# Expert products scattered in float32, one slot buffer, and a second late ring buffer

## The chip, the cores and the metric

The kernel runs on one core of one Trainium2 chip. The metric is the device time of one execution in microseconds (us). Before the change it is 1568.03 us, the median of three runs (1567.27 to 1569.21).

## The reference

Four transformer layers are computed for 256 tokens of width 1024. The first two layers (`first_block`) have a token mixer and a mixture of 32 experts; the last two (`second_block`) have other mixers and a dense feed-forward part. The change touches the experts of the first two layers alone:

```python
def hierarchical_moe(h, w_grp, b_grp, w_exp, b_exp, w_gate, w_up, w_down):
    ...
    g_idx = jnp.argmax(grp_logits, axis=-1)
    ...
    top_logit, top_idx = lax.top_k(in_grp, TOP_K)          # TOP_K = 2 of 8 experts of one group
    weights = jax.nn.softmax(top_logit, axis=-1) * p_grp
    expert_id = g_idx[:, None] * EXPERTS_PER_GROUP + top_idx
    combine = ...                                          # token x 32 experts, two non-zero per token
    for gi in range(N_GROUPS):
        hid = silu(t @ w_gate[e]) * (t @ w_up[e])          # for the 8 experts e of the group
        y = y + (hid * combine[e]) @ w_down[e]
```

Each expert has a gate matrix and an up matrix of 1024 x 256 and a down matrix of 256 x 1024, 1 MB each in float32. One layer so reads 96 MB of expert weights.

## The kernel before

**Experts.** Each expert gets 32 slots (`CAP`), and four experts make a block of 128 slots. `moe` walks over nine blocks, `BLOCKS = 0..6, "x", 7`; block "x" gives 32 more slots to the expert with the most tokens. For a block, `slots` picks the tokens with one-hot matmuls (`gp`, evicted by ACT into `xsl`), `gate_up` runs the gate and up products (L1095, tile `gu`, 32-row tiles of four experts side by side) and makes `P`, the one-hot matrix slots x tokens (L1106). `turn` transposes the hidden values (`hdt`, `hT`), `down` runs the down products (L1136, tile `dn`, two halves of 512 columns), and `scatter` adds them at their tokens with matmuls against `P` into four accumulators `ya` (L1153). The last lines of `moe` add `ya` to the residual `x` on DVE (L1188).

**The scatter's precision.** `down` splits each half of `dn` in two parts of type float32r: ACT copies the half into `ys0` (L1140), and DVE writes the remainder `dn - ys0` into `ys1` (L1141). `scatter` runs one float32r matmul for each part, so two for each of the eight slices `k` of 128 columns. In the trace a float32r matmul is one MATMUL record and a float32 matmul is two: the 1024 float32 matmuls of L1095 with the tile `xsl` are listed x2048, and the 288 float32r ones of L1153 x288. Each record is called a pass here.

**The ring of weight buffers.** All weights come through one in-order list of DMAs on SP (class `Ring`, L213), 1 MB each as a rule. A DMA is issued when a buffer is free. There are 8 base buffers and 3 more; during the experts of a layer come `NX` = 6 more from the space of the mixer, and `NY` = 1 more (`extend(1, NY, there)`), once the projection before the experts has given up its space. That is 18. The list goes, for the experts, gate x4, up x4 of block 0, gate x4, up x4 of block 1, down x4 of block 0, and so on.

**Order of the work.** The engines' queues are filled by a scheduler at build time, which interleaves the matmuls of neighbouring steps. `overflow` stands under a test on the device for the case that an expert has more tokens than slots; it is skipped in the profiled execution (no instruction of its body is in the trace), but every engine reads the count and takes the branch (L1194, L1195), between block 6 and block "x".

**Space.** The pool of a layer's experts has tags with a number of buffers each: `k1=3`, `k2=2`, `x4=2`, `k8=1`. `x4` holds `xsl`, 4 KB a partition for each buffer; a ring buffer takes 8 KB a partition.

Of the kernel before, what the change touches and what calls it, by code (L numbers as in the profile page):

```python
# [10 lines left out]
F32 = mybir.dt.float32  # L11
R32 = mybir.dt.float32r
U32 = mybir.dt.uint32
I32 = mybir.dt.int32
AF = mybir.ActivationFunctionType
# [11 lines left out]
NB = 8  # L27
NM = 3
NX = 6
NY = 1  # L30
LAST = 2, 3
K2 = 9
K3 = 2
# [195 lines left out]
class K:  # L229
# [791 lines left out]
    def moe(self, l, ps, sb, gate, last):  # L1021
# [64 lines left out]
        def gate_up(b, info, xs):  # L1086
            es = members(b)
            n = CAP * len(es)
            gu = ps.tile([128, 2, 256], F32, name="gu", tag="ps")
            for m, name in enumerate(("mg", "mu")):  # L1090
                w = [self.W.get((name, l, e)).rearrange("p (k f) -> p k f", k=KD) for e in es]
                for k in range(KD):
                    for j in range(len(es)):
                        q = slice(CAP * j, CAP * j + CAP)
                        nc.tensor.matmul(gu[q, m], xs[:, k, q], w[j][:, k],  # L1095
                                         start=k == 0 and m == 0, stop=k == KD - 1 and m == 1,
                                         tile_position=(0, CAP * j))
                for e in es:
                    self.W.done((name, l, e))
            inf = info() if callable(info) else info  # L1100
            sg = sb.tile([128, 256], F32, name="sg", tag="k1")
            nc.scalar.activation(sg[:n], gu[:n, 0], AF.Silu)  # L1102
            hid = sg
            nc.vector.scalar_tensor_tensor(hid[:n], sg[:n], inf[:, 1:2], gu[:n, 1], op0=OP.mult, op1=OP.mult)  # L1104
            P = sb.tile([128, T], R32, name="P", bufs=3)
            nc.vector.tensor_scalar(P[:n], c("iota1")[:n], inf[:, 0:1], None, op0=OP.is_equal)  # L1106
            Ps[b] = P
            return hid
# [9 lines left out]
        def down(b, halves=(0, 1)):  # L1118
# [7 lines left out]
                keys = [[("md", l, e) for e in es]] * 2  # L1126
                w = [[self.W.get(k)[:, 1024 * n:1024 * n + 1024] for k in keys[0]] for n in range(2)]
            if 0 in halves:
                ys[b] = [sb.tile([128, KD, 128], R32, name=f"ys{j}", bufs=1) for j in range(2)]
            y = ys[b]  # L1130
            for n in halves:
                dn = ps.tile([128, 512], F32, name="dn", tag="ps")
# [4 lines left out]
                                         start=j == 0, stop=j == 1, tile_position=(0, CAP * i))  # L1137
                v = dn[:m].rearrange("s (k p) -> s k p", k=4)
                s = slice(4 * n, 4 * n + 4)
                nc.scalar.activation(y[0][:m, s], v, AF.Copy)  # L1140
                nc.vector.tensor_tensor(y[1][:m, s], v, y[0][:m, s], op=OP.subtract)  # L1141
                if b == 7:
                    for k in dict.fromkeys(keys[n]):
                        self.W.done(k)
# [4 lines left out]
        def scatter(b, ks=range(KD)):  # L1149
            m = CAP * len(members(b))  # L1150
            for k in ks:
                for j in range(2):
                    nc.tensor.matmul(ya[k // 2][:, k % 2], ys[b][j][:m, k], Ps[b][:m],  # L1153
                                     start=b == BLOCKS[0] and j == 0 and k % 2 == 0,
                                     stop=b == BLOCKS[-1] and j == 1 and k % 2 == 1)

        cur = slots(0)
        most, cap, number, px, wx = weights()
# [32 lines left out]
    def overflow(self, l, ps, sb, ht, tw, place, most, cap, ya):  # L1191
# [3 lines left out]
        with self.tc.If(n > 0):  # L1195
# [6 lines left out]
            ov = sb.tile([128, 2, 32], F32, name="ov")  # L1202
            nc.vector.tensor_tensor(ov, place, cap.unsqueeze(1).to_broadcast([128, 2, 32]), op=OP.is_gt)
            nc.vector.tensor_tensor(ov, ov, tw[:, :, 1:], op=OP.mult)
            hid = sb.tile([128, 2, T], F32, name="ohid", tag="x4")

            def part(src):
                t = sb.tile([128, 512], F32, name="ow", tag="k2")
# [1 line left out]
                return t  # L1210

            for e in range(NE):
                wb = ps.tile([128, T], F32, name="wb", tag="ps")
                for cc in range(2):
                    nc.tensor.matmul(wb[:, 128 * cc:128 * cc + 128], ov[:, cc, e:e + 1].to_broadcast([128, 128]),
                                     c("ident"), start=True, stop=True)
                gu = [ps.tile([128, 2, T], F32, name="ogu", tag="ps") for _ in range(2)]
                for m, name in enumerate(("wg", "wu")):
                    src = self.A[name][l, e].rearrange("(p k) f -> p (k f)", p=128)
                    for k in range(KD):  # L1220
                        if k % 2 == 0:
                            v = part(src[:, 256 * k:256 * k + 512]).rearrange("p (k j f) -> p k j f", k=2, j=2)
                        for j in range(2):
                            nc.tensor.matmul(gu[m][:, j], v[:, k % 2, j], h(k), start=k == 0 and j == 0,
                                             stop=k == KD - 1 and j == 1)
                nc.scalar.activation(hid, gu[0], AF.Silu)
                nc.vector.tensor_tensor(hid, hid, gu[1], op=OP.mult)
                nc.vector.tensor_tensor(hid, hid, wb.unsqueeze(1).to_broadcast([128, 2, T]), op=OP.mult)
                for n in range(2):
                    for j in range(2):  # L1230
                        o = 1024 * n + 512 * j
                        v = part(self.A["wd"][l, e][:, o:o + 512]).rearrange("f (k p) -> f k p", k=4)
                        for k in range(4):
                            nc.tensor.matmul(ya[2 * n + k // 2][:, k % 2], v[:, k], hid[:, j], start=False, stop=False)

    def final_norm(self, ps, sb, sc, sh, hl):

# [262 lines left out]
    def run(self, out):  # L1500
# [26 lines left out]
        for l in range(2):  # L1527
# [36 lines left out]
            self.out_proj(ps, ("wout", l), self.hl, gate, self.router(l, ps))  # L1564
            self.split.close()
            assert not self.chunks and not self.parts
            es, sb = self.phase(f"moe{l}", there, k1=3, k2=2, x4=2, k8=1)
            if NY:
                extend(1, NY, there)
            gate = mlp_gate  # L1570
# [307 lines left out]
```

## Time and profile before

| | us |
|---|---|
| median of three runs | 1568.03 |
| lowest, highest | 1567.27, 1569.21 |
| the profiled execution, whole | 1566.22 |
| its span, first to last instruction | 1564.1 |
| PE busy (matmul) | 1447.1 |
| DVE busy | 824.1 |
| ACT busy | 656.1 |

The experts of the first layer lie at 221 to 445 us of the span, those of the second at 647 to 871 us. [...] PE busy is no measure of how full PE is, since matmuls overlap; a timeline row that starts after the one ahead of it has ended shows an idle PE, and in square brackets what ended the idle time.

### The profile page before, as it was taken

To read this page: it belongs to the slowest core of one execution; us is meant where nothing else is said; L and a number is where in the kernel's file an instruction comes from. 1 tells how busy PE (TensorE), PEld (TensorE's weight loads), DVE (VectorE), ACT (ScalarE), POOL (GpSimd) and SP (SyncE) were. 2 spreads that over 40 slices of the span, in tenths; PEclk is the share of its full clock that TensorE was granted. 3 is DMA by queue.
4 is the path that set the end of the run, shared out by engine and by line. 5 is a ranking of instruction groups with operands and counts; after the bars stand their busy time and mean duration, and the time that the engine had idled before them with its cause. 6 is when DMAs were issued, how large, how long until landed. Compare 5 with 4: busy or idle time off the path is not lost. (4 is left out here: it accounts for less than half of the span.)

```text
span 1564.1 us, 28414 instructions
## 1 busy us (share of the span) xinstructions
PE 1447.1 (93%) x11988; PEld 1143.9 (73%) x11988; DVE 824.1 (53%) x1580; ACT 656.1 (42%) x1098; POOL 3.0 (0%) x11
## 2 busy tenths in 40 slices
PE   4999999878989999897889999999999999899997
PEld 2868876434457778754445688799996997799996
DVE  3585631100157755311011667888846675788853
ACT  3534522111144254321121486566634544466643
POOL 0000000000000000000000000000000000000000
PEclk8999999989989999999899999999999999999999
DMA  9976789999998368899999877955546644655520
GB/s 379 420 278 243 277 326 421 421 421 420 416 393 348 121 243 329 333 420 420 421 420 415 335 291 283 375 190 186 176 159 245 244 162 157 221 193 185 189 82 28
DMA packets 64954, 453.02 MB, mean 290 GB/s; under 512 B 7088, under 2 KB 7728, under 8 KB 11440
## 3 DMA queue, kind: packets, MB, share of 16 engines
q1 hardware_dynamic: 63520, 446.94, 73.5%
q10 hardware_dynamic: 1296, 4.15, 0.7%
q8 instruction: 98, 1.61, 0.4%
q14 instruction: 40, 0.33, 0.1%
HBM read 450.01 MB, written 1.05 MB: 288 GB/s over the span
## 5 line engine op out<-in xcount | busy, mean ns | idle before, releaser
L517 PE MATMUL pj<-act,wh 128*128 128x256 f32 x3136 | 582.1, 287 | 20.3 <-ACT act L464 12.6
L517 PEld LDWEIGHTS pj<-act,wh 128*128 128x128 f32 x3136 | 494.8, 194 | 55.9 <-ACT act L464 15.3
L517 PE MATMUL pj<-act,wl 128*128 128x256 f32 x1568 | 446.2, 285 | 0.6 <-DVE wl L510 0.6
L510 DVE TENSOR_TENSOR wl<-wt,wh 128x1024 fp32r<-128x1024 f32 x260 | 317.2, 1223 | 222.7 <-ACT wh L509 220.0
L509 ACT ACTIVATE wh<-wt 128x1024 fp32r<-128x1024 f32 x260 | 274.3, 1059 | 345.8 <-PE pj L517 269.4
L517 PEld LDWEIGHTS pj<-act,wl 128*128 128x128 f32 x1568 | 303.3, 193 | 3.0 <-issue 1.2
L1095 PE MATMUL gu<-wt,xsl 128*32 128x256 f32 x2048 | 148.5, 410 | 36.8 <-DMA wt<-in_wu 33.8
L1095 PEld LDWEIGHTS gu<-wt,xsl 128*32 128x32 f32 x2048 | 72.4, 117 | 103.2 <-DMA wt<-in_wu 44.9
L517 PE MATMUL fd<-F,wh 128*128 128x256 f32 x704 | 125.0, 281 | 0.0
L1136 PE MATMUL dn<-wt,hT 128*32 128x512 f32 x528 | 114.5, 613 | 0.9 <-ACT hT L1116 0.9
L299 PE MATMUL ad<-wt,cz 128*32 128x512 f32 x768 | 112.9, 614 | 0.0
L517 PEld LDWEIGHTS fd<-F,wh 128*128 128x128 f32 x704 | 107.8, 188 | 0.2 <-ACT wh L509 0.2
L1104 DVE SCALAR_TENSOR_TENSOR sg<-sg,inf,gu 128x256 f32<-128x256 f32 x16 | 7.7, 480 | 180.6 <-ACT sg L1102 180.5
L517 PE MATMUL fd<-F,wl 128*128 128x256 f32 x352 | 98.6, 281 | 0.0
L1102 ACT ACTIVATE sg<-gu 128x256 f32<-128x256 f32 (+1 forms) x18 | 6.9, 382 | 212.5 <-PE gu L1095 206.1
L567 DVE SCALAR_TENSOR_TENSOR u<-pj,par,u 128x255 f32<-128x255 f32 (+1 forms) x176 | 84.3, 479 | 3.0
L1058 ACT ACTIVATE xsl<-gp,mod,gsm 128x128 f32<-128x128 f32 x128 | 48.1, 456 | 57.0 <-PE gp L1055 57.0
L1055 PEld LDWEIGHTS gp<-G,ht 128*128 128x128 f32 x512 | 62.2, 200 | 11.0 <-issue 11.0
L1055 PE MATMUL gp<-G,ht 128*128 128x128 f32 x512 | 65.7, 285 | 1.6 <-DVE G L1033 1.6
L517 PEld LDWEIGHTS fd<-F,wl 128*128 128x128 f32 x352 | 66.3, 188 | 0.0
L1136 PEld LDWEIGHTS dn<-wt,hT 128*32 128x32 f32 x528 | 26.4, 111 | 51.7 <-issue 43.2
L1153 PEld LDWEIGHTS ya<-P,ys 128*128 128x128 f32 (+1 forms) x288 | 36.9, 188 | 28.7 <-issue 12.8
(395 smaller groups left out, 1524.0 us busy)
## 6 DMA issues: line engine op xcount, KB each, us to landing
wt<-in_ada SPq DMA_DIRECT2D x96, 1024.0 KB, 6.9
wt<-in_wg SPq DMA_DIRECT2D x66, 1024.0 KB, 19.8
wt<-in_wu SPq DMA_DIRECT2D x66, 1024.0 KB, 19.8
wt<-in_wd SPq DMA_DIRECT2D x66, 1024.0 KB, 19.8
wt<-in_fup SPq DMA_DIRECT2D x44, 1024.0 KB, 4.9
wt<-in_win SPq DMA_DIRECT2D x26, 1024.0 KB, 12.9
wt<-in_fdn SPq DMA_DIRECT2D x22, 1024.0 KB, 4.8
wt<-in_glain SPq DMA_DIRECT2D x12, 1024.0 KB, 6.9
```

The source lines that it names most:

```text
L299: nc.tensor.matmul(acc[32 * g:32 * g + 32], cz[:, k, :], w[:, 512 * g:512 * g + 512], start=k % 4 == 0, stop=k % 4 == 3, tile_position=(0, ...
L509: nc.scalar.activation(wh, raw, AF.Copy)
L510: nc.vector.tensor_tensor(wl, raw, wh, op=OP.subtract)
L517: nc.tensor.matmul(out, lhs[a], rhs[b], start=first and i == 0, stop=last and i == 2)
L567: nc.vector.scalar_tensor_tensor(out[:, d:], src[:, :T - d], w(taps - 1 - d), out[:, d:], op0=OP.mult, op1=OP.add)
L1055: nc.tensor.matmul(gp[:, kk], ht[:, k + kk, cc], G[:, cc].rearrange("p a b -> p (a b)"), start=kk == 0 and cc == 0, stop=kk == 3 and cc == 1)
L1058: nc.scalar.activation(xs[:, kk], gp[:, kk - k], AF.Identity, scale=self.gs[:, kk:kk + 1], bias=self.sh[:, kk:kk + 1])
L1095: nc.tensor.matmul(gu[q, m], xs[:, k, q], w[j][:, k], start=k == 0 and m == 0, stop=k == KD - 1 and m == 1, tile_position=(0, CAP * j))
L1102: nc.scalar.activation(sg[:n], gu[:n, 0], AF.Silu)
L1104: nc.vector.scalar_tensor_tensor(hid[:n], sg[:n], inf[:, 1:2], gu[:n, 1], op0=OP.mult, op1=OP.mult)
L1136: nc.tensor.matmul(dn[q], hT[b][:, j, q], w[n][i][:, 512 * j:512 * j + 512], start=j == 0, stop=j == 1, tile_position=(0, CAP * i))
L1153: nc.tensor.matmul(ya[k // 2][:, k % 2], ys[b][j][:m, k], Ps[b][:m], start=b == BLOCKS[0] and j == 0 and k % 2 == 0, stop=b == BLOCKS[-1] ...
```

## The change

The down products are kept as one float32 tile `ys` (4 KB a partition in place of two tiles of 4 KB), half of each bank copied by ACT and half by DVE. `P` becomes float32, and `scatter` runs one float32 matmul for each slice in place of two float32r ones. The tag `x4` goes from two buffers to one. `NY` goes from 1 to 2, which makes 19 ring buffers during the experts. In the skipped `overflow` the hidden tile moves to a tag of 1 KB a partition, and its loops run over halves of the tokens; that part is cut here.

```diff
-NY = 1
+NY = 2
...
-            P = sb.tile([128, T], R32, name="P", bufs=3)
+            P = sb.tile([128, T], F32, name="P", bufs=3)
...
-                ys[b] = [sb.tile([128, KD, 128], R32, name=f"ys{j}", bufs=1) for j in range(2)]
+                ys[b] = sb.tile([128, KD, 128], F32, name="ys", bufs=1)
...
-                nc.scalar.activation(y[0][:m, s], v, AF.Copy)
-                nc.vector.tensor_tensor(y[1][:m, s], v, y[0][:m, s], op=OP.subtract)
+                nc.scalar.activation(y[:m, s][:, :2], v[:, :2], AF.Copy)
+                nc.vector.tensor_copy(y[:m, s][:, 2:], v[:, 2:])
...
             for k in ks:
-                for j in range(2):
-                    nc.tensor.matmul(ya[k // 2][:, k % 2], ys[b][j][:m, k], Ps[b][:m],
-                                     start=b == BLOCKS[0] and j == 0 and k % 2 == 0,
-                                     stop=b == BLOCKS[-1] and j == 1 and k % 2 == 1)
+                nc.tensor.matmul(ya[k // 2][:, k % 2], ys[b][:m, k], Ps[b][:m], start=b == BLOCKS[0] and k % 2 == 0,
+                                 stop=b == BLOCKS[-1] and k % 2 == 1)
...
-            hid = sb.tile([128, 2, T], F32, name="ohid", tag="x4")
+            hid = sb.tile([128, 2, 128], F32, name="ohid", tag="k1")
...
-            es, sb = self.phase(f"moe{l}", there, k1=3, k2=2, x4=2, k8=1)
+            es, sb = self.phase(f"moe{l}", there, k1=3, k2=2, x4=1, k8=1)
```

How the queues stand, at three places of the first layer (the second has the same ones).

SP, the loads just before and after the first gate and up products (`wt` are ring buffers; in brackets the engines and DMA queues whose signals a load waits for). Before:

```order
L213 DMA wt_2056<-in_wu 128x2048 [waits DMAHW5_49,PE_49]
L213 DMA wt_2062<-in_wu 128x2048 [waits DMAHW6_49]
L213 DMA wt_2071<-in_wu 128x2048 [waits DMAHW7_49,PE_49]
L213 DMA wt_2077<-in_wu 128x2048 [waits DMAHW0_49,PE_49]
L213 DMA wt_2083<-in_wd 128x2048 [waits DMAHW1_49,PE_49]
L213 DMA wt_2151<-in_wd 128x2048 [waits DMAHW2_49,PE_49]
L213 DMA wt_2255<-in_wd 128x2048 [waits DMAHW3_49,PE_49]
L213 DMA wt_2257<-in_wd 128x2048 [waits DMAHW4_49,PE_49]
```

SP, the same loads with the change:

```order
L213 DMA wt_2056<-in_wu 128x2048 [waits DMAHW5_49,PE_49]
L213 DMA wt_2058<-in_wu 128x2048 [waits DMAHW6_49]
L213 DMA wt_2064<-in_wu 128x2048 [waits DMAHW7_49]
L213 DMA wt_2073<-in_wu 128x2048 [waits DMAHW0_49,PE_49]
L213 DMA wt_2079<-in_wd 128x2048 [waits DMAHW1_49,PE_49]
L213 DMA wt_2085<-in_wd 128x2048 [waits DMAHW2_49,PE_49]
L213 DMA wt_2153<-in_wd 128x2048 [waits DMAHW3_49,PE_49]
L213 DMA wt_2257<-in_wd 128x2048 [waits DMAHW4_49,PE_49]
```

The third load needs no signal of PE now, since the second late buffer is there for it, and each load behind it takes the release that the one behind it took before; two buffers (2255, 2257) were handed out after the first gate products before, and one (2257) now.

PE, the last down products and scatters, from the second half of block 7 on. Before:

```order
L1136 MATMUL dn<-wt_6122,hT 32x512
L1153 MATMUL ya<-P,ys_6269 128x256 x2
L1136 MATMUL dn<-wt_6122,hT 32x512
L1136 MATMUL dn<-wt_6124,hT 32x512 x2
L1136 MATMUL dn<-wt_6122,hT 32x512
L1153 MATMUL ya<-P,ys_6270 128x256
L1153 MATMUL ya<-P,ys_6269 128x256
L1153 MATMUL ya<-P,ys_6270 128x256 x2
L1153 MATMUL ya<-P,ys_6269 128x256
L1153 MATMUL ya<-P,ys_6270 128x256
L1136 MATMUL dn<-wt_6122,hT 32x512
L1136 MATMUL dn<-wt_6124,hT 32x512 x2
```

PE, with the change, from the transpose of block 7 to the end of its scatter:

```order
L1114 MATMUL hdt<-cst_71,sg 128x128 x2
L1136 MATMUL dn<-wt_3327,hT 32x512 x2
L1136 MATMUL dn<-wt_3329,hT 32x512 x2
L1136 MATMUL dn<-wt_3327,hT 32x512 x2
L1136 MATMUL dn<-wt_3329,hT 32x512 x2
L1136 MATMUL dn<-wt_8563,hT 32x512
L1152 MATMUL ya<-P,ys 128x256 x4
L1136 MATMUL dn<-wt_8563,hT 32x512
L1136 MATMUL dn<-wt_8565,hT 32x512 x2
L1136 MATMUL dn<-wt_8563,hT 32x512 x2
L1136 MATMUL dn<-wt_8565,hT 32x512 x2
L1152 MATMUL ya<-P,ys 128x256 x4
```

The first half's scatter is one piece of four float32 matmuls (eight passes) where two pieces of float32r matmuls stood on both sides of three down products, and the second half's scatter is four matmuls.

ACT, the end of the experts and the start of the next norm (`warm` is a small activation behind the load of a function table, `nsq` the squares for the norm). Before:

```order
L1116 ACTIVATE hT<-hdt 128x256 [waits PE_49]
L1140 ACTIVATE ys_6269<-dn 128x512 [waits DVE_49,PE_49]
L1140 ACTIVATE ys_6269<-dn 128x512 [waits PE_49]
L412 ACT_TABLE_LOAD
L412 ACTIVATE warm<-x,eps 128x1 [waits DVE_49]
```

ACT, with the change:

```order
L1116 ACTIVATE hT<-hdt 128x256 [waits PE_49]
L1140 ACTIVATE ys<-dn 128x256 [waits DVE_49,PE_49]
L412 ACT_TABLE_LOAD
L412 ACTIVATE warm<-x,eps 128x1 [waits DVE_49]
L1140 ACTIVATE ys<-dn 128x256 [waits PE_49]
```

The table load and `warm` now stand between the two copies of block 7. DVE's copies of the other halves, with the change, wait for ACT:

```order
L1104 SCALAR_TENSOR_TENSOR sg<-sg,inf,gu 128x256 [waits Activation_49]
L1141 COPY ys<-dn 128x256 [waits Activation_49]
L1186 SCALAR_TENSOR_TENSOR x<-ya,mod_171,x 128x256 [waits PE_49]
L1186 SCALAR_TENSOR_TENSOR x<-ya,mod_171,x 128x256
L1186 SCALAR_TENSOR_TENSOR x<-ya,mod_171,x 128x256 [waits PE_49]
```

## Rows read from the trace of the kernel before

**Rows 1.** Stretches of 10 us: five engines busy, clock, DMA share, GB/s.
```profile
310.00:320.00 10.00, 4.94 (x56) 2.05 (x52) 0.00 (x0) 0.00 (x0) 0.00 (x0) 0.87 1.01 419
...
820.00:830.00 10.00, 10.00 (x52) 5.44 (x51) 1.67 (x4) 0.60 (x1) 0.00 (x0) 0.66 1.02 424
```
**Rows 2.** SP's waits at the first gate products, both layers: us, times, longest.
```profile
SPq L213 <- PE gu L1095: 12.6, 1, 12.6
...
SPq L213 <- PE gu L1095: 10.5, 1, 10.5
```
**Rows 3.** One stretch of 1 us, columns as in Rows 1.
```profile
226.00:227.00 1.00, 1.00 (x19) 0.60 (x21) 0.00 (x0) 0.72 (x3) 0.00 (x0) 1.00 0.06 25
```
**Rows 4.** PE's timeline at the last waits for weights, both layers.
```profile
379.02 5.03 PE L1095 MATMUL gu<-wt,xsl 128*32 128x256 f32 x57 [1.51 <-DMA wt<-in_wu]
...
803.83 5.95 PE L1095 MATMUL gu<-wt,xsl 128*32 128x256 f32 x57 [1.89 <-DMA wt<-in_wu]
```
**Rows 5.** PE's timeline from the branch to block 7, first layer.
```profile
404.79 0.35 PE L1153 MATMUL ya<-P,ys 128*128 128x256 f32 x1 [3.40 <-PEq L1195]
405.07 8.78 PE L1095 MATMUL gu<-wt,xsx 128*32 128x256 f32 x32
413.78 2.05 PE L1153 MATMUL ya<-P,ys 128*128 128x256 f32 x15
415.76 3.64 PE L1136 MATMUL dn<-wt,hT 128*32 128x512 f32 x32
...
419.57 1.46 PE L1153 MATMUL ya<-P,ys 128*128 128x256 f32 x10
420.95 1.04 PE L1136 MATMUL dn<-wt,hT 128*32 128x512 f32 x2
...
432.44 2.16 PE L1153 MATMUL ya<-P,ys 32*128 32x256 f32 x16
```
**Rows 6.** PE's timeline, second layer: block 7, then the next norm.
```profile
863.81 0.50 PE L1153 MATMUL ya<-P,ys 128*128 128x256 f32 x2
864.24 1.06 PE L1136 MATMUL dn<-wt,hT 128*32 128x512 f32 x8
865.24 0.98 PE L1153 MATMUL ya<-P,ys 128*128 128x256 f32 x6
866.14 1.06 PE L1136 MATMUL dn<-wt,hT 128*32 128x512 f32 x6
867.13 1.05 PE L311 MATMUL adt<-cst,adrow 128*128 128x4 f32 x8
...
870.36 1.16 PE L381 MATMUL nm<-nsq,fin 128*32 128x256 f32 x6 [0.72 <-ACT nsq L416]
...
875.11 1.03 PE L384 MATMUL nm<-nsq,cst 128*128 128x256 f32 x4
875.97 1.03 PE L384 MATMUL nm<-nsq,fin 128*128 128x256 f32 x4
```
**Rows 7.** Timeline at the end of the first layer's experts, ACT and PE.
```profile
441.61 0.60 ACT L1140 ACTIVATE ys<-dn 128x512 fp32r<-128x512 f32 x1 [3.56 <-PE dn L1136]
442.23 1.28 ACT L412 ACT_TABLE_LOAD   x1
...
442.26 0.51 PE L1153 MATMUL ya<-P,ys 128*128 128x256 f32 x2 [0.73 <-ACT ys L1140]
...
444.68 0.63 PE L381 MATMUL nm<-nsq,cst 128*32 128x256 f32 x4 [0.72 <-ACT nsq L416]
```
**Rows 8.** Groups by form: busy us, mean ns of one | idle before.
```profile
L1141 DVE TENSOR_TENSOR ys<-dn,ys 128x512 fp32r<-128x512 f32 x32 | 22.1, 692 | 47.8 <-ACT ys L1140 47.8
L1116 ACT ACTIVATE hT<-hdt 128x256 f32<-128x256 f32 x16 | 6.1, 383 | 23.9 <-PE hdt L1114 23.9
```
**Rows 9.** The branch L1195 by engine: count, ns min/median/max, first and last start.
```profile
L1195 PEldq COMPARE_BRANCH x2: 6059/6089/6119, 398.5 to 824.8; - x2
```
**Rows 10.** PE's timeline behind the branch, second layer.
```profile
832.45 1.89 PE L1095 MATMUL gu<-wt,xsx 128*32 128x256 f32 x8 [1.07 <-DVEq L1195]
```

More of the change, by code (lines that the diff above doesn't have):

```diff
@@ L1212, in overflow @@
             for e in range(NE):
-                wb = ps.tile([128, T], F32, name="wb", tag="ps")
                 for cc in range(2):
[L1215 to L1222, printed above, removed]
-                        for j in range(2):
-                            nc.tensor.matmul(gu[m][:, j], v[:, k % 2, j], h(k), start=k == 0 and j == 0,
-                                             stop=k == KD - 1 and j == 1)
@@ L1226, in overflow @@
[L1226 to L1234, printed above, removed]
+                    t = slice(128 * cc, 128 * cc + 128)
@@ new lines, in overflow @@
+                    wb = ps.tile([128, 128], F32, name="wb", tag="ps")
+                    nc.tensor.matmul(wb, ov[:, cc, e:e + 1].to_broadcast([128, 128]), c("ident"), start=True, stop=True)
+                    gu = [ps.tile([128, 2, 128], F32, name="ogu", tag="ps") for _ in range(2)]
+                    for m, name in enumerate(("wg", "wu")):
+                        src = self.A[name][l, e].rearrange("(p k) f -> p (k f)", p=128)
+                        for k in range(KD):
+                            if k % 2 == 0:
+                                v = part(src[:, 256 * k:256 * k + 512]).rearrange("p (k j f) -> p k j f", k=2, j=2)
+                            for j in range(2):
+                                nc.tensor.matmul(gu[m][:, j], v[:, k % 2, j], h(k)[:, t], start=k == 0 and j == 0,
+                                                 stop=k == KD - 1 and j == 1)
@@ new lines, in overflow @@
+                    nc.scalar.activation(hid, gu[0], AF.Silu)
+                    nc.vector.tensor_tensor(hid, hid, gu[1], op=OP.mult)
+                    nc.vector.tensor_tensor(hid, hid, wb.unsqueeze(1).to_broadcast([128, 2, 128]), op=OP.mult)
+                    for n in range(2):
+                        for j in range(2):
+                            o = 1024 * n + 512 * j
+                            v = part(self.A["wd"][l, e][:, o:o + 512]).rearrange("f (k p) -> f k p", k=4)
+                            for k in range(4):
+                                nc.tensor.matmul(ya[2 * n + k // 2][:, k % 2, t], v[:, k], hid[:, j], start=False,
+                                                 stop=False)
```

## The prediction

> **What bounds the kernel now.** I read the stretches of 10 us first, to find which engine is full where the experts run, then SP's waits, then PE's timeline through the experts' end. The change touches the experts of two layers and nothing else, so their stretches are all that counts. In the middle of a layer's experts the DMA engines are full (share 1.01, 419 GB/s), and PE is busy for 4.94 of 10 us [rows 1]: the loads set the pace. That ends with the last load that PE waits for, the up weights of block 6. PE waits for one at 379.02 us and at 803.83 us for the last time in each layer [rows 4]. From there on PE's rows follow each other nearly without a hole: the branch, block "x", the scatters of blocks 5, 6 and "x", and block 7 [rows 5, 6]. So a layer's experts have three parts. At first PE works on what was loaded ahead; then the loads decide; and in the last 65 us PE decides, with the short chain ACT, DVE, PE at the end [rows 7]. A saving or a cost counts in full if it moves the last awaited load, or lies in PE's last part.
>
> **The buffer.** SP waits 12.6 us in the first layer and 10.5 us in the second for PE to release the first gate buffers [rows 2], and the DMA engines run dry meanwhile (share 0.06 in a stretch of that time [rows 3]). Six loads go out between the end of the projection and that release now. The order of SP's queue shows a seventh with the change: the third load needs no signal of PE any more, and all behind it move up by one release. One load of 1.05 MB at 419 GB/s [rows 1] is 2.5 us. Nothing dries up after that point, so each later load lands one load earlier, the last awaited one too: 2.5 us for each layer, **5.0 us gained**. The bounds are 0, if the queue stays empty for as long all the same, and 2.5 us for each layer, since one buffer can't bring more than one load. I take the upper one, because the empty time in the rows (12.6 and 10.5 us of waiting) is longer than a load.
>
> **The scatter.** A float32r matmul is one pass, and a float32 one is two. The nearest row for a float32 pass of 128 x 256 over all 128 rows is in the next norm: four passes of L384 start 0.86 us before the next four [rows 6], 0.215 us each. Sixteen passes, so one block's scatter, cost 3.44 us. Before, they cost what the starts of the rows that follow show [rows 5, 6]:
>
> Block 5: 0.28 us for the first (404.79 to 405.07) and 1.98 us for fifteen (413.78 to 415.76), 2.26 us; more by 1.18 us.
> Block 6: 1.38 us for ten (419.57 to 420.95) and six as in 865.24 to 866.14, 0.90 us; more by 1.16 us.
> Block "x": 2.16 us; more by 1.28 us.
> Block 7, first half: 0.43 us (863.81 to 864.24) and 0.90 us; eight passes now cost 1.72 us, more by 0.39 us.
>
> That is 4.0 us for each layer in PE's last part, and the shapes repeat in both, so **8.0 us lost**. [...] The scatters of blocks 0 to 4 get longer by the same 1.2 us each, some 6 us a layer. They cost nothing as long as PE idles for half of the time there [rows 1]; without that cover they would cost 12 us in all.
>
> **The end of the chain.** The second half of block 7 was: down products end (0.08 us before 441.61), ACT copies 0.60 us, PE starts the scatter at 442.26, ACT loads a table for 1.28 us, and PE starts the sums for the norm at 444.68 us, after 0.72 us of waiting for ACT's squares [rows 7]. That is 3.15 us from the end of the down products. Now ACT copies 128 x 256 of it, half of the tile, in 0.38 us by the nearest row [rows 8]. The table load stands ahead of it, where ACT idled for 3.56 us [rows 7], so it is covered, and the squares of the first four slices are ready before PE has ended its scatter. PE needs 0.08 + 0.38 + 0.05 us to start and 1.72 us for eight passes, 2.23 us. So the sums start **0.9 us** earlier in the first layer. If `warm`, which waits for the first slice of `x`, were late, ACT's copy would be late behind it, and the gain would be gone. In the second layer PE does the turn of a row (`adt`) first: it ends near 868.1 us, the scatter would end at 869.8, and the sums started at 870.36 [rows 6]: **0.5 us** gained.
>
> **DVE's copy and the branch.** DVE copied the remainder for 692 ns [rows 8] after ACT's 597; now it copies a half. The order shows that this copy waits for ACT, so the two halves run one after the other, 0.38 and some 0.35 to 0.45 us in place of 0.60 and 0.69: 0.5 us less ahead of the branch. In the first layer that hides: PE's own branch takes 6.06 us [rows 9] and lets PE start at 404.79, later than DVE. In the second PE waits 1.07 us for DVE's branch [rows 10], so **0.5 us** are gained there.
>
> [...]
>
> [...]
>
> **At nothing.** One buffer for `xsl` in place of two: the next block's products into it stand behind the gate and up products of this block in PE's queue in both orders, so no engine waits more. `P` in float32 has the same size. The skipped body of `overflow` gets longer, which costs nothing unless the 6.06 us of the branch depend on the distance. One pair of loads changes places in the second mixer, where PE waits for no load.
>
> **The sum.** -5.0 + 8.0 - 0.9 - 0.5 - 0.5 = +1.1 us. The profiled execution took 1566.2 us, so it would take 1567.3; the median of the runs lies 1.8 us above it, which makes **1569.1 us**. A measurement of this kernel can tell about 0.2%, 3.1 us, from no change, so this is no change.
>
> **Rivals.**
> *The lead is lost (slower).* The place is SP's queue ahead of the first gate products. If the added load waits for the same release as before, or if the loads behind it start later by as much, the last awaited load lands when it did, and the scatters' cost stays: +1.1 + 5.0, so 1574.1 us, 0.4% slower. It decides if fewer than seven loads go out before that release. For it: the order names only engines that a load waits for, not which of their instructions. Against it: the buffer handed out after the first products is one now, where it was two.
> *The clock stays up (faster).* PE runs at half speed after some waits: the last 57 up products take 5.03 and 5.95 us [rows 4], where four experts side by side at 0.215 us would need 3.1 us (57 / 4 x 0.215), and the 32 products behind the branch, of one expert and so one after the other, take 8.7 us [rows 5], 0.27 us each against 0.215. In 820 to 830 us the clock is at 0.66 though PE is busy all the time [rows 1]. These stretches cost some 1.9, 2.8, 1.8 and 3.4 us, 9.9 us in all. More passes mean fewer holes. If half of it went, 5.0 us would be gained: 1564.1 us. Against it: the holes before the last awaited load shrink from about 5 to 4 us only, and where a drop falls may turn out worse as well.
> *The middle scatters show too.* If PE falls behind the loads, all eighteen scatters count: 12 us more, 1581 us. Against it stands the idle half of PE in [rows 1].
>
> **How the numbers follow.** The forecast has a chance of 0.52, the lost lead 0.20, the clock 0.18, the middle scatters 0.05, and 0.05 is left for what I don't see. Within 0.2% means 1564.9 to 1571.2 us. Most of the forecast lies in it (0.46 of 0.52), and 0.04 of the rest: same 0.50. Slower gets the lost lead, the middle scatters and 0.05 more: 0.30. Faster gets most of the clock's chance and some of the rest: 0.20. The range runs from the clock's case to the lost lead's, 1564 to 1574.5 us.
>
> **What would show it.** In the trace after, seven loads before the first gate products, the last wait for up weights 2.5 us earlier against the start of the experts, passes of L1152 at 0.215 us, one scatter of 3.4 us for each of the blocks 5, 6 and "x", and the sums for the norm 2.2 us behind the last down products. The prediction is wrong if that last wait hasn't moved, if PE waits for a load behind it, or if half-speed stretches in the last part differ by more than 3 us in sum from those before.

## The result: 1% slower, far outside the range

The changed kernel takes 1584.2 us (median of four runs, 1577.9 to 1585.9) against 1567.7 us for the kernel before (four runs): a ratio of 1.0097, 95% interval 1.008 to 1.0114. The forecast was 1569.1 us, the range ended at 1574.5 us. The profiled execution has a span of 1581.1 us, 17.0 us more than before.

Where the 17 us came from is read by marks that both traces have: the first rank products of a layer (`rkp`, they start its experts), the last up products that wait for weights, and the first sums for the next norm.

Rank products on PE's timeline of the kernel before (start us, us, ...), both layers:
```profile
218.71 0.38 PE L970 MATMUL rkp<-oh,cst 128*128 128x32 f32 x2 [1.82 <-DVE w L984]
...
644.79 0.38 PE L970 MATMUL rkp<-oh,cst 128*128 128x32 f32 x2 [1.30 <-DVE w L984]
```
The same marks in the changed kernel, with the last waits for weights and the sums for the norm:
```profile
221.19 0.38 PE L970 MATMUL rkp<-oh,cst 128*128 128x32 f32 x2 [1.83 <-DVE w L984]
...
379.27 5.92 PE L1095 MATMUL gu<-wt,xsl 128*32 128x256 f32 x57 [1.87 <-DMA wt<-in_wu]
...
453.45 0.62 PE L381 MATMUL nm<-nsq,cst 128*32 128x256 f32 x4 [0.72 <-ACT nsq L416]
...
653.63 0.38 PE L970 MATMUL rkp<-oh,cst 128*128 128x32 f32 x2 [1.30 <-DVE w L984]
...
809.82 5.68 PE L1095 MATMUL gu<-wt,xsl 128*32 128x256 f32 x57 [1.65 <-DMA wt<-in_wu]
...
888.63 0.62 PE L381 MATMUL nm<-nsq,fin 128*32 128x256 f32 x4 [0.72 <-ACT nsq L416]
```
With [rows 4, 6, 7] for the kernel before, the differences of these starts are:

| stretch | before | after | change |
|---|---|---|---|
| start to the first layer's rank products | 218.7 | 221.2 | +2.5 |
| first layer: rank products to the last awaited weights | 160.3 | 158.1 | -2.2 |
| first layer: from there to the sums for the norm | 65.7 | 74.2 | +8.5 |
| up to the second layer's rank products | 200.1 | 200.2 | +0.1 |
| second layer: to the last awaited weights | 159.0 | 156.2 | -2.9 |
| second layer: from there to the sums for the norm | 66.5 | 78.8 | +12.3 |
| to the end of the span | 693.7 | 692.5 | -1.3 |

So the lead is there, 5.1 us for both layers, and the loss is in PE's last part, where +3 us were forecast for each layer (4.0 for the passes, less the end of the chain and the branch). Two things in that part weren't in the sum.

**A hole behind the branch.** PE's timeline of the changed kernel in the second layer, from the scatter of block 5 on:
```profile
837.02 0.46 PE L1152 MATMUL ya<-P,ys 128*128 128x256 f32 x1 [0.82 <-PEq L1193]
842.70 0.59 PE L1152 MATMUL ya<-P,ys 128*128 128x256 f32 x1 [5.23 <-issue]
843.22 9.71 PE L1095 MATMUL gu<-wt,xsx 128*32 128x256 f32 x32
```
The branch has ended, one pass of the first scatter has run, and its second pass comes 5.23 us later. "Issue" means that the profile shows nothing that it waits for. Block x's products then take 9.7 us, in good part at half speed (granted clock 0.50 from 843 to 848 us, below), where 7.1 us are enough at full speed (a row of the run with the shift, below).

**The clock.** Stretches of the kernel before: both last parts, and block x's scatter with 6 us behind it (us, engines busy, granted clock with 1.00 as full speed, DMA share, GB/s):
```profile
379.02:444.68 65.66, 59.84 (x464) 31.74 (x464) 12.01 (x28) 12.04 (x26) 0.52 (x1) 0.95 1.02 417
803.83:870.36 66.53, 63.26 (x473) 33.58 (x473) 12.09 (x29) 12.04 (x26) 0.00 (x0) 0.91 1.02 418
432.00:440.00 8.00, 7.53 (x55) 3.71 (x51) 1.17 (x2) 1.36 (x3) 0.00 (x0) 1.00 1.03 415
```
The same of the changed kernel, with 8 us up to the fall, the fall beside block x's scatter, and the one behind the hole:
```profile
379.27:453.45 74.18, 70.78 (x464) 37.03 (x464) 10.46 (x29) 10.33 (x26) 0.52 (x1) 0.87 1.01 418
809.82:888.63 78.81, 71.29 (x472) 38.19 (x473) 10.54 (x30) 10.33 (x26) 0.00 (x0) 0.88 0.88 352
431.00:439.00 8.00, 8.00 (x107) 5.38 (x96) 0.48 (x1) 0.38 (x1) 0.00 (x0) 1.00 1.03 415
439.00:445.00 6.00, 5.53 (x22) 1.71 (x21) 0.00 (x0) 0.38 (x1) 0.00 (x0) 0.50 1.01 419
...
843.00:848.00 5.00, 5.00 (x13) 2.00 (x13) 0.00 (x0) 0.00 (x0) 0.00 (x0) 0.50 1.03 426
```
A stretch times what is missing of its clock is an estimate of what the clock took, and an upper one, since an idle PE loses nothing by it: 3.3 and 6.0 us before, 9.6 and 9.5 us after, so up to 9.8 us more. One fall is plain to see: at 439 us, 3 us after block x's scatter began, the clock goes from 1.00 to 0.50, though PE had been busy without a gap for 8 us.

### The profile page after: what moved, and what is told of

Its sections match the earlier page's. It is cut to its first block, busy times and chain, and to the rows that moved or that the text cites. A ratio compares the mean times of both kernels' runs of the same rounds, so it can differ in the third digit from the quotient of the medians.

```text
span 1581.1 us, 28422 instructions
## 1 busy us (share of the span) xinstructions
PE 1475.3 (93%) x11988; PEld 1160.9 (73%) x11988; DVE 815.1 (52%) x1580; ACT 648.1 (41%) x1098; POOL 3.0 (0%) x11
## 3 DMA queue, kind: packets, MB, share of 16 engines
q8 instruction: 99, 1.62, 0.4%
## 5 line engine op out<-in xcount | busy, mean ns | idle before, releaser
L510 DVE TENSOR_TENSOR wl<-wt,wh 128x1024 fp32r<-128x1024 f32 x260 | 317.4, 1224 | 221.9 <-ACT wh L509 219.0
L1095 PE MATMUL gu<-wt,xsl 128*32 128x256 f32 x2048 | 144.9, 413 | 22.7 <-DMA wt<-in_wu 22.7
L1136 PE MATMUL dn<-wt,hT 128*32 128x512 f32 x528 | 119.8, 643 | 0.9 <-ACT hT L1116 0.9
L1152 PE MATMUL ya<-P,ys 128*128 128x256 f32 (+1 forms) x288 | 71.7, 394 | 7.6 <-issue 5.2
L1152 PEld LDWEIGHTS ya<-P,ys 128*128 128x128 f32 (+1 forms) x288 | 52.3, 190 | 26.3 <-ACT ys L1140 12.0
```

The source lines that it names most:

```text
L510: nc.vector.tensor_tensor(wl, raw, wh, op=OP.subtract)
L1095: nc.tensor.matmul(gu[q, m], xs[:, k, q], w[j][:, k], start=k == 0 and m == 0, stop=k == KD - 1 and m == 1, tile_position=(0, CAP * j))
L1136: nc.tensor.matmul(dn[q], hT[b][:, j, q], w[n][i][:, 512 * j:512 * j + 512], start=j == 0, stop=j == 1, tile_position=(0, CAP * i))
L1152: nc.tensor.matmul(ya[k // 2][:, k % 2], ys[b][:m, k], Ps[b][:m], start=b == BLOCKS[0] and k % 2 == 0, stop=b == BLOCKS[-1] and k % 2 == 1)
```

## Experiments

The kernel before was run beside these and took 1567.7 to 1568.4 us in three groups of 19 to 21 runs, so the times of different groups can be compared to about 1 us.

**The changed kernel again.** No edit.

> The changed kernel once more, nothing altered. Its trace so far shows 17 us more span than before: 2.5 us ahead of the first experts, where no instruction differs; 6.3 us in the first layer's experts; 9.4 us in the second's, of which 5.23 us are a hole right behind the skipped overflow, in which PE waits for nothing that the profile shows. Theory 'place in the code': the hole belongs to how the longer overflow body lies in PE's program, so it stands at the same scatter again, 4.5 to 6 us, in the second layer only; time 1580 to 1586 us. Theory 'chance': the hole is gone or in another layer, and the runs spread by some 8 us as the first four did (1577.9 to 1585.9 us). The 2.5 us at the start should be gone if they were chance.

1583.1 us (six runs, 1577.6 to 1593.8; before 1568.4 in 19 runs). The hole is in the second layer again, at the same pass:
```profile
837.80 0.45 PE L1152 MATMUL ya<-P,ys 128*128 128x256 f32 x1 [1.05 <-PEq L1193]
843.92 0.59 PE L1152 MATMUL ya<-P,ys 128*128 128x256 f32 x1 [5.66 <-issue]
```
So it belongs to the program and not to chance. The first rank products come at 221.9 us (221.2 in the first trace), so the late start did not go either.

PE's rows name nothing that it waits for, but the DMA queues have transfers that fit. Two queues are of the kind "instruction"; over the whole span of the changed kernel the profile's page has of the larger one, q8 (packets, MB, share of 16 engines):
```profile
q8 instruction: 99, 1.62, 0.4%
```
That is 16.4 KB for each transfer. Near the branch of the second layer they start at 834.3 and at 840.0 us (one more at 846.4). The row of the quarter of a microsecond at 840.00:
```profile
q8 instruction: 1, 0.02, 27.9%
```
The branch ends 2.5 us after the first of these starts, and the hole ends 2.7 us after the second. In the first layer transfers start at 404.3 and 410.0 us; there PE leaves the branch 2.5 us after the first, and no such hole follows (block x's products start at 407.98 us and take 7.07 us). That q8 carries PE's program no view shows; it is the author's estimate from shares. Of the 1.96 MB that the two instruction queues moved, q8 has 1.62 MB, or 83%; of the trace's 28422 instructions PE has 11988 matmuls and as many weight loads, or 84%. Behind a branch of 6 us, the second transfer starts 5.7 to 6.0 us after the first in the first traces of both kernels (two layers each), and 5.5 to 6.0 us, read in steps of a quarter of a microsecond, in the second layer of seven further traces.

**A short body.**
```diff
-            for e in range(NE):
+            for e in range(1):
```


> The changed kernel with the loop of the skipped overflow cut from 32 experts to one, so that its body is some 30 times shorter in every engine's program; the timed data never enter it. Theory 'the branch pays for the distance': PE's compare-and-branch falls from 6.1 us to well under 1 us, the 5.23 us hole goes too, PE starts block x some 1.4 us earlier in the first layer and 6 to 7 us earlier in the second: 1572 to 1577 us. Theory 'a branch costs 6 us wherever it goes': 6.1 us again and a time within 2 us of the changed kernel's, unless the hole goes with the other place in the program (then 5 us less).

1577.2 us (eight runs), 6 us less than the changed kernel, and no hole; the time lies at the edge of the first theory's, the branches fit neither theory. PE's branch, both layers (ns min/median/max, first and last start):
```profile
L1193 PEldq COMPARE_BRANCH  x2: 525/3408/6290, 399.2 to 829.4; - x2
```
It takes 0.5 us in the first layer and 6.3 us in the second, with the same short jump. So a jump is not paid by its length alone. In the first layer a transfer of q8 starts at 397.3 us, ahead of the branch (399.2 us); in the second one starts at 833.0 us, inside the branch (829.4 to 835.7 us). That what counts is whether the target is already there is the author's reading of these times. The hole went in both theories of that run, so it takes another run (the same jump, other places) to tell them apart.

**Without the lead.** `NY = 1`, all else of the change.

> The changed kernel with NY = 1, so 18 ring buffers: float32 scatter, new copies, one slot buffer, no lead. Theory 'the lead works': the last awaited up weights come 2.2 to 2.9 us later in each layer against the start of the experts than in the changed kernel, and the time is some 5 us longer, 1587 to 1590 us. Rival 'the lead costs' (the loads that run ahead collide with something else): the time is the changed kernel's or below it.

1588.5 us (six runs), 5.4 us more than the changed kernel. From the rank products to the last awaited weights it is 159.0 us in both layers, against 158.0 and 156.3 us in the second trace of the changed kernel: 1.0 and 2.7 us, where 2.2 to 2.9 us were expected in each layer. The lead works, less in the first layer than in the second. The trace has a trap, behind the branch of the second layer:
```profile
840.18 0.67 PE L1152 MATMUL ya<-P,ys 128*128 128x256 f32 x2 [0.70 <-PEq L1193]
845.90 4.36 PE L1095 MATMUL gu<-wt,xsx 128*32 128x256 f32 x13 [5.05 <-DMA wt<-in_wg]
```
The idle time is put down to a load of gate weights. It is the same hole, one pass later: transfers of q8 start at 837.5 and 843.2 us, and PE goes on 2.7 us behind the second, as before.

**The lead alone.** `NY = 2` and `x4=1` as in the change, down products and scatter as before it, and room made for them:
```diff
-        self.wr = mid.tile([128, KD, 64], F32, name="wrt")
+        self.wr = mid.tile([128, KD, 36], F32, name="wrt")
...
-        oh, tw, t8 = small("oh", 32), small("tw", 33), small("t8", 4, 8)
+        oh, tw, t8 = small("oh", 32), small("tw", 33), el
...
-                t = sb.tile([128, 512], F32, name="ow", tag="k2")
+                t = sb.tile([128, 256], F32, name="ow", tag="k2")
```


> The lead without the float32 scatter: NY = 2 and one slot buffer as in the changed kernel, but the down products split in two float32r parts and scattered in two passes for each slice as before. The room comes from 36 router columns in place of 64, from 1 KB tiles in the skipped overflow, and from reused tiles of the router; the skipped body is again longer than before's. Theory 'scatter and holes cost, the lead gains': the last awaited loads come 2.2 to 2.9 us earlier than before in each layer, and the time is 4 to 6 us below before's, 1562 to 1564 us, or 5 us above that if the hole behind the branch goes with the longer body. Rival 'the lead costs': no faster than before, 1568 us or more.

1571.3 us (12 runs), 11.8 us less than the changed kernel. Both have the lead and a hole, so that is about what the float32 scatter costs with all that hangs on it; what the narrower router tiles do to the time no run shows by itself. The hole is here 6.12 us:
```profile
817.35 6.18 PE L1137 MATMUL dn<-wt,hT 128*32 128x512 f32 x20
829.66 0.37 PE L1154 MATMUL ya<-P,ys 128*128 128x256 f32 x1 [6.12 <-issue]
```
That is the case of 1562 to 1564 us with some 5 us for the hole, and 2 us more than that.

**The same jump, other places.** The loop of the first layer's skipped body is one expert shorter; the second layer's own body is unchanged.
```diff
-            for e in range(NE):
+            for e in range(NE - (l == 0)):
```


> The changed kernel with one of 32 experts left out of the skipped overflow of the first layer only, so that all that stands behind it in the programs lies some hundred instructions earlier, while the second layer's own skipped body, and so the length of its jump, is unchanged. The first runs showed the hole at the same place in the second layer (5.23 and 5.66 us) with three instruction transfers of 16 KB about it (at 834, 840 and 846 us) where the first layer has two. Theory 'the jump lands near the end of a 16 KB piece of program': the hole goes from the second layer, which keeps its one branch of 6 us: some 5 us less than the changed kernel, 1578 us. Rival 'the longer jump costs it': the hole stays, 1583 us.

The hole is gone, with the second layer's branch as long as before (831.8 us on, 6.1 us):
```profile
838.09 0.67 PE L1152 MATMUL ya<-P,ys 128*128 128x256 f32 x2 [1.09 <-PEq L1193]
838.77 7.07 PE L1095 MATMUL gu<-wt,xsx 128*32 128x256 f32 x32
845.77 3.29 PE L1152 MATMUL ya<-P,ys 128*128 128x256 f32 x14
```
Transfers start at 835.4 and 841.1 us: PE has done 3 us of work since the branch when the second one starts, and doesn't stop. So the hole hangs on where the code lies, not on the length of the jump. That the target lies near the end of a piece of 16 KB, the size of a transfer, is an estimate that fits the transfers; no view shows the place itself. In the five traces of this document that have a hole, one more transfer starts within 0.6 us of the branch's own start (831.0 beside 830.9 us in the changed kernel), and in no other: the shift moves the branch and its target together, and no run tells the two apart.

The time is 1581.4 us (five runs, 1576.3 to 1586.1), only 1.7 us less than the changed kernel's 1583.1 us, where 5 us less were expected. The second layer's last part takes 73.8 us in place of 78.8 us. That would be less still, but the clock now fell for some 7 us beside block x's scatter (4.50 us for it, where it takes 3.72 at full speed); in the three traces with the hole and the float32 scatter over 32 rows it fell there for 3.4 us or not at all. The rest was lost in parts that the edit doesn't touch: 2.5 us more than in the first trace of the changed kernel lie behind the second layer's experts.

**Block x over 128 rows.**
```diff
+            if b == "x":
+                nc.gpsimd.memset(P[32:64], 0.0)
+                nc.gpsimd.memset(P[64:128], 0.0)
...
+                if b == "x":
+                    nc.gpsimd.memset(ys[b][32:64], 0.0)
+                    nc.gpsimd.memset(ys[b][64:128], 0.0)
...
-            m = CAP * len(members(b))
+            m = 128
```


> The changed kernel with the scatter of block x over 128 rows, 96 of them zeros that GpSimd writes, in place of 32 rows; the same sixteen passes. In all four traces with the float32 scatter the granted clock of the first layer falls to 0.5 about 3 us after this scatter begins, and stays there for 7 us (3.4 us lost); in the two traces with float32r it does not. Theory 'PE is thinly used while only 32 rows are fed, for 3.65 us now and 2.1 us before': the fall at that place is gone in both layers, 3 to 5 us less than the changed kernel, 1578 to 1580 us. Rival 'the fall comes from the thin products of block x before it, or by chance': it stays, at the same place, 1583 us.

1581.2 us (five runs, 1577.0 to 1583.3), only 1.9 us less than the changed kernel, where 3 to 5 us were expected. No fall beside the scatter in either layer. PE's timeline and a stretch of the first layer:
```profile
435.39 3.72 PE L1158 MATMUL ya<-P,ys 128*128 128x256 f32 x16
438.95 0.38 PE L1117 MATMUL hdt<-cst,sg 128*128 128x128 f32 x2
```
```profile
434.00:447.00 13.00, 12.01 (x81) 6.51 (x77) 2.81 (x7) 3.11 (x6) 0.00 (x0) 1.00 1.02 419
```
The first layer's last part takes 69.0 us in place of 74.2. Part of that is another fall, at 398 us, that this trace doesn't have; the hole of the second layer is there (5.30 us). But in this trace the experts start 2.9 us later (224.1 us), and the second layer's last awaited weights come 3.0 us later (159.2 us behind the rank products in place of 156.2), which takes back most of the gain. With float32 over 32 rows the clock falls within 2 to 5 us of the scatter's start in nine of ten cases (five traces, two layers; in the tenth, the second layer of the changed kernel's first trace, not): in seven during the scatter, in two 0.3 and 1.2 us behind its end. With float32r over 32 rows, 2.1 us long, it does so in two of fourteen; over 128 rows in none of four (the last two are of the next run).

**Both repairs.** The edits of the last two runs together.

> The changed kernel with both repairs: the first layer's skipped body one expert shorter (the hole in the second layer went with that) and block x's scatter over 128 rows (the fall of the clock beside it went with that). If hole and clock are two causes that add up, the time is some 5.5 us (hole) and 3 to 4 us (clock) under the changed kernel's 1583 us: 1573 to 1576 us, and what is left over the kernel before is the price of the passes less the lead: twice 4.7 us and some 0.5 us at the end of each chain, less 5 us, so about 1573.5 us. Rival 'a third cause': 1578 us or more.

1571.6 us (eleven runs), 1.0024 times the kernel before (1.0008 to 1.0041), 3.8 us more than it, and a little below the 1573 to 1576 us expected: a third cause of that size isn't needed. The changed kernel takes 11.5 us more than this: that is what the two causes come to together. The single repairs gained 1.7 and 1.9 us, so their times don't add up to it; five runs each, spread over 6 to 10 us, leave open what each is worth alone. Both last parts, with the columns as above:
```profile
377.96:448.87 70.91, 67.56 (x464) 36.51 (x464) 10.45 (x29) 10.35 (x26) 2.42 (x3) 0.92 1.02 418
805.07:875.80 70.73, 68.15 (x473) 37.54 (x473) 10.54 (x30) 10.35 (x26) 1.89 (x2) 0.92 0.98 393
```

**The lead alone, with the shift.** The run of the lead alone with the first layer's body one expert shorter.

> The lead with the float32r scatter (as in the run of the lead alone, 1571.3 us with a hole of 6.12 us behind the branch of the second layer), with the first layer's skipped body one expert shorter so that the second layer's code lies elsewhere. Theory 'place in the code': the hole is gone, 1564 to 1566 us, some 3 us under the kernel before. Rival 'the lead does not pay': 1568 us or more with no hole left.

1561.6 us (eleven runs), 0.9966 times the kernel before (0.9948 to 0.9983): faster than both kernels, and below the 1564 to 1566 us expected. PE's timeline behind the branch of the second layer shows the hole gone:
```profile
828.02 0.35 PE L1154 MATMUL ya<-P,ys 128*128 128x256 f32 x1 [0.51 <-PEq L1196]
829.57 7.07 PE L1096 MATMUL gu<-wt,xsx 128*32 128x256 f32 x32 [1.20 <-DMA wt<-in_wg]
```
The 1.20 us that are left are put down to a load, but DVE comes out of its branch at 829.2 us: it is mainly the wait for DVE that the kernel before has there too, 1.07 us [rows 10].

**The control for the shift.** The kernel before with the same edit.

> The kernel before, nothing changed but one expert left out of the first layer's skipped overflow, as a control for the runs with that edit. If the edit matters only through where the second layer's code lies, the branch takes 6 us as before and the time is 1567 to 1569 us, or 5 to 6 us more if the jump now lands at the end of a piece of program (a hole behind the branch then shows in the second layer). Rival 'the edit itself gains': below 1565 us, and the gain of the lead with that edit (1561.6 us) would not be the lead's.

1569.4 us (eleven runs), 1.0013 times the kernel before (1.0 to 1.0027). The shift gains nothing by itself. So the 6 us come with the lead, or with the narrower router tiles that made room for it, which no run has alone; in the trace 3.6 and 1.2 us of them lie between the rank products and the last awaited weights, and none ahead of the experts.

**An earlier branch.** The lead alone, with the test moved into the loads' part:
```diff
-                self.overflow(l, ps, sb, ht, tw, place, most, cap, ya)
...
+            if b == 3:
+                self.overflow(l, ps, sb, ht, tw, place, most, cap, ya)
```


> The lead with the float32r scatter and the test for overflow moved from behind block 6 to behind block 3, where PE waits for loads for half of its time; the skipped body reads the tokens without overwriting them, so it may stand there. Theory 'PE pays for its program after a jump only where it is the bound': the branch still takes 6 us, the last awaited up weights do not move, and the 3.4 to 1.0 us in front of block x, the wait for DVE's branch and the hole are gone: 1558 to 1563 us. Rival 'the branch breaks up the order of the work, or holds the loads up': the last awaited weights come later by what the branch takes, 1568 us or more.

1568.2 us (eleven runs), 0.9986 times the kernel before (0.9968 to 1.0004): no gain. The rival's time came, though not by late loads: the last awaited weights come 155.0 us after the rank products in the first layer, as early as in the run of the lead alone, and PE waits for no branch behind block 6. But the branch had also kept the scheduler from mixing what stands on both sides of it. Without it, block x's scatter goes ahead of block 7's products, and block 7 has nothing left to cover its own chain:
```profile
432.19 0.44 PE L1115 MATMUL hdt<-cst,sg 128*128 128x128 f32 x2 [1.03 <-DVE sg L1105]
433.10 1.93 PE L1137 MATMUL dn<-wt,hT 128*32 128x512 f32 x16 [0.47 <-ACT hT L1117]
435.77 0.50 PE L1154 MATMUL ya<-P,ys 128*128 128x256 f32 x2 [0.74 <-ACT ys L1141]
```
The last parts take 68.0 and 71.5 us, 2.5 and 4.0 us more than in the run with the shift.

**The kernel before, twice more.** No edit.

> The kernel before once more, for a second trace of it. Two things rest on its single trace. First, the first experts start at 218.7 us there and, in the ten traces with other code from the first layer's experts on, at 219.5 to 224.1 us, though the code ahead of them is the same: if that is chance, this trace starts them anywhere from 218 to 224 us; if it belongs to the code, below 219 us. Second, block x's scatter: with two float32r passes over 32 rows the granted clock stays at 1.00 in the first layer; if the fall beside that scatter belongs to its length, it is absent here too.

> The kernel before a third time, as in the run ahead: experts of the first layer from below 219 us if their start belongs to the code, from 218 to 224 us if it is chance; no fall of the clock beside block x's scatter in the first layer, and no hole behind the branch of the second layer.

1566.2 and 1570.2 us. The rank products of the first layer come at 218.72 and 218.59 us. So all four traces with the code of before (the control for the shift is the fourth) have 218.5 to 218.7 us, and the ten others 219.5 to 224.1 us. That is hardly chance; why, stays open. Part of it is seen in the first load: the nine issues of `ada` weights that open SP's queue take 8.7 to 9.3 us in those four and 9.7 to 10.3 us in nine of the ten others (8.7 us in the run with the earlier branch, which starts its experts first of the ten), and PE's first projection starts up to 2.8 us later, though in the changed kernel no instruction ahead of the experts differs. The other part is one more fall of the clock in the first mixer in some of them (to 0.50 at 91 us, for 3.4 us in the second trace of the changed kernel and in the run with the shift, for 6.8 us in the run over 128 rows). No hole behind the branch in either; beside block x's scatter the clock fell in the first layer of the second of these two traces, for 3.4 us, against what was expected, and not in the other.

## Why the prediction was wrong

The changed kernel took 15.1 us more than forecast. What took it out of the range is a term put at nothing, the longer skipped body, and the clock, which was a rival with the wrong sign: without the hole and the fall beside block x's scatter it takes 1571.6 us, inside the range. Two terms of the sum were mis-sized besides, the passes and the end of the chain.

**What bounds the kernel: right.** The loads decide up to the last awaited weights, PE behind them.

**The buffer: right.** 5.0 us were forecast, 2.2 and 2.9 us were measured in the trace, 5.4 us by taking it back (1.0 and 2.7 us of them up to the last awaited weights, so the first layer got less of it). SP's timeline has the seven loads: they go out at 211.6 to 219.4 us, ahead of the wait for the first gate products, where six did at 209.2 to 217.0 us. The rival of the lost lead (0.20) falls.

**The scatter: too low.** 0.215 us for a pass was read from a row of four; sixteen in a row take 3.65 us, 0.228 each. In the changed kernel, block 6 of the first layer and what follows:
```profile
422.00 3.72 PE L1152 MATMUL ya<-P,ys 128*128 128x256 f32 x16
425.65 3.19 PE L1136 MATMUL dn<-wt,hT 128*32 128x512 f32 x7
```
By the second layer of the run with both repairs, where nothing disturbs them, blocks 5, 6, x and the first half of 7 cost 1.4, 1.4, 1.5 and 0.6 us more than before, 4.9 us for a layer where 4.0 were forecast: 9.7 in place of 8.0. The scatters of blocks 0 to 4 cost nothing, as forecast, nor did the single slot buffer: without the lead it is 159.0 us to the last awaited weights in both layers, against 160.3 and 159.0 us before.

**The end of the chain: wrong.** 0.9 and 0.5 us were to be gained. From ACT's copy to the sums for the norm it is 3.07 us before [rows 7] and 3.15 us after; in the second layer, from the turn of `adt`, 3.23 [rows 6] and 3.61 us. The step that failed here is that the squares of the first four slices would be ready before PE has ended its scatter. ACT on the timeline of the changed kernel:
```profile
450.30 0.38 ACT L1140 ACTIVATE ys<-dn 128x256 f32<-128x256 f32 x1 [1.94 <-PE dn L1136]
...
452.77 1.67 ACT L416 ACTIVATE nsq<-x 128x512 f32<-128x512 f32 x3 [2.08 <-PE ya L1152]
```
The first square waits for the last pass of the scatter, before as after: the 0.72 us that PE waits for it stand behind the scatter in both [rows 7]. The wait was in those rows, and was read as if the table load had caused it. The copy ends 0.2 us sooner, and the passes take 0.3 us more.

**DVE's copy and the branch: right in size.** In the second layer of the run with both repairs PE has 0.9 us from the first scatter's start to block x's products, where it had 1.43 before (831.02 to 832.45 us): 0.5 us gained. In the changed kernel the hole hid it. In the first layer DVE's branch no longer hides in full: PE waits 0.4 us for it there.

**At nothing: wrong.** "The skipped body gets longer, which costs nothing unless the 6.06 us of the branch depend on the distance" asked the wrong question. The branch takes 6.0 to 6.2 us as before; what counts is where the code lies, since the hole of 5.2 to 5.7 us went with one expert fewer in the first layer's body. That it hangs on how much of the program lies between the target and the end of a piece of 16 KB is the author's estimate from the transfers, and not shown. The longer body moved the second layer's code so that PE stands still for 5.2 to 5.7 us, and with the fall of the clock that followed, block x's products take 2.6 us more (9.7 against 7.1). No cover was named for that, since no cost was seen.

**The clock: a rival with the wrong sign.** It was named as a gain of 5.0 us (0.18), because more passes leave fewer holes; that a drop may turn out worse was said, and not priced. The granted clock took up to 9.8 us more in the two last parts, and the prediction's own sign of being wrong was 3 us. A PE without a hole is not enough: beside 3.65 us of passes over 32 of 128 rows it fell in nine of ten cases, in seven of them while PE was busy. It wasn't all of that in time, since a slower PE arrives later at the branch and then waits less for it: in the first layer the 20 down products ahead of it take 6.1 us in place of 3.6, and the wait is 1.0 us in place of 3.4.

With hole and fall taken away the change costs 3.8 us, where the sum had 1.1. The two mis-sized terms, the passes (1.7 us) and the end of the chain (1.9 us), make 3.6 us. In the trace that is about what is missing: its two last parts take 9.5 us more than before, where 6.1 us were forecast. In the median it is more than the 2.7 us that are missing there, and the late start adds to that. What goes the other way is the clock of the whole execution: 0.967 on average over the eleven executions with both repairs and 0.964 over the 21 of the kernel before beside them, some 4 us. Whether that is the change's doing isn't settled.

## What to carry to other kernels

A skipped body isn't free: here PE's jump over it took 6 us and ended 2.5 us behind the start of a transfer in the queue "instruction", and in some places of the code PE stood still a second time, for 5.1 to 6.1 us. A change of a body that never runs so cost some 5 us of PE's time, and a control that only shifts the code tells it apart from what the change does. Look for such a stop in that queue too, since the profile put it down to "issue" (5.23 us) or to a load (5.05 us). Doubling the passes of a matmul over few rows cost more than the passes where the clock fell beside them (sixteen took 4.50 us, and 3.72 at full speed); zeros in the other rows cost no pass and kept it up there in all four cases (1.00 from 434 to 447 us in one of them). And a wait that a profile names in the row ahead of an edit (ACT for PE, 0.72 us) is to be followed to its releaser before the edit is credited with removing it.

## What the runs showed of the hardware

- A compare-and-branch on PE took 5.9 to 6.3 us over a skipped body in the eight traces where its row was read, but for one layer of the short body (0.5 us); on ACT and DVE the same branch took 45 to 72 ns.
- Behind a branch of 6 us, the second transfer of 16 KB in the queue "instruction" started 5.5 to 6.0 us after the first, and PE went on 2.4 to 2.9 us behind the start of one of them.
- In the five traces with a hole of 5.1 to 6.1 us behind the branch the granted clock fell to 0.50 in the hole (at 841.7 us in the changed kernel), and block x's products behind it were slow: 9.7 us in place of 7.1 there, 8.5 us in the lead alone.
- The granted clock fell from 1.00 to 0.50 in the middle of unbroken matmuls, some 3 us into float32 passes that fed 32 of 128 rows (seven of ten cases; 439.0 us in the first layer of the changed kernel, 2.9 us in); with the other rows fed zeros it did not (four cases).
